# The opening of a hybrid decoder step: the next channel tile's modulation in three operations and ahead of the second block, and a residual load named later

## The chip, the cores and the metric

The kernel runs on one core of one Trainium2 chip. The metric is the device time of one launch in microseconds (us). Before the change it is 2659.37 us, the median of 3 runs that lie between 2658.36 and 2660.74.

The engines are TensorE (PE), VectorE (DVE), ScalarE (ACT), GpSimd (POOL) and SyncE (SP). In this kernel SP issues the loads and stores, all on one queue.

## The reference

One layer for a prompt of 2048 tokens and a sample group of 8 x 8 tokens, 1024 channels, in float32. Cut to what matters:

```python
mod = einsum('bd,de->be', silu(c), w_ada) + b_ada          # c: 1 prompt row, 8 sample rows
sh1, sc1, g1, sh2, sc2, g2 = split(mod, 6)
h = rmsnorm(x, norm_mix_w) * (1 + sc1) + sh1
proj = h @ w_in                                            # q k v z b a | sliding window q k v
o_dn  = gated_deltanet(proj[...])                          # short convolution first, then chunks of 64
o_swa = window_attention(proj[...])
x = x + g1 * (concat(o_dn, o_swa) @ w_out)
h = rmsnorm(x, norm_ffn_w) * (1 + sc2) + sh2
u = causal_conv3(h @ ffn_w_up) + ffn_conv_b
x = x + g2 * ((silu(gate(u)) * up(u)) @ ffn_w_down)
y = rmsnorm(x, final_norm_w)
```

The six vectors `sh1 ... g2` are the modulation; the code numbers them as components 0 to 5. Component 1 enters as `(1 + sc1) * norm_mix_w`, component 0 as an added term.

## The kernel before, in words

**Layout.** Activations stand transposed, channels on the 128 partitions in 8 channel tiles, tokens along the free dimension in blocks of up to 512. The first half of the tokens has the blocks 0 and 1, of 512 each. A product in near-float32 precision is made of three products of rounded parts: an operand is split into `hi` and `lo` (weights: `split`, L329 to L333, w_hi on ACT, w_lo on VectorE L332), and for each channel tile TensorE takes hi·w_hi, lo·w_hi and hi·w_lo (L340).

**Stages in time.** The opening (to about 70 us) computes the modulation components 0 and 1, the norm of blocks 0 and 1, and the first two column tiles of the input projection. To about 395 us follow the other columns of that projection beside components 2 to 5, to about 690 us the DeltaNet and attention mixers of the first half, then the second half, output projection, FFN up and FFN down.

**A modulation step** (`ada_load` L165, `ada_cols` L174). For one channel tile k the two 512 KB pieces of `w_ada` (components 1 and 0) are loaded, through six buffers (`WADA`). TensorE multiplies them with silu(c) (L182, `ada_ps`, the projection), ACT copies the result (L185, `ms`), TensorE transposes it (L189, `adat_ps`), and VectorE adds up four partial sums (L196) and the bias (L197) for each of the two components, and for component 1 adds 1 (L199) and multiplies by the norm's weight (L200). `ada_cols` is a generator: its first `next` makes projection and copy, the rest makes transposes and VectorE's part.

**What takes the modulation** (`affine_h`, L241). For each block and channel tile VectorE computes ht = x · S · rstd (L265). For block 0 ACT adds the shift and rounds to hi (L271), VectorE makes lo (L272). For block 1 ACT adds the shift (L267), rounds (L268), and POOL makes lo (L269).

**The norm** (`first_rstd` L296, `token_rstd` L206). ACT squares x (L302), VectorE adds tiles up (L304, L309), TensorE sums over partitions (L215, `ss_ps`), VectorE and POOL take the inverse root (L144, L145), VectorE makes diagonals (L219, `dg`), TensorE spreads the result over the partitions (L223, `rb_ps`), ACT copies it (L225, `sg`).

**The opening's loop** (L1943 on). Block 0's norm and tile 0's modulation come first. Then for each k the loop starts the loads of a further tile, `next(ada[k + 1])` (projection of tile k + 1), the steps that `PLAN[k]` lists (2: one channel tile of block 0 through `first_two`; 1: a step of block 1's norm; 3: a channel tile of block 1), and `rest(ada[k + 1])`. After it come constants (`in_consts`, L570): loads of `cw` and `dnw` (L573), the scaling of `dnw` by 0.5 on VectorE (L574), and the load of `cout` (L577). These three loads are issued behind the last `w_ada` load. POOL's copy `sb` (L553) reads what lands with `cout`.

**FFN down** (`down_phase`, L1642). In it `load_x` (L1810, load at L1816) fetches tiles of the residual; it is called in steps 1 and 5 of a phase (L1831).

**What sets the order.** The program text is the input of a scheduler that simulates the engines and writes a fixed list of instructions for each engine and for the queue. Each engine takes its list in order; an instruction that waits holds all behind it on its engine. So the source order decides only indirectly.

Of the kernel before, what the change touches and what calls it, by code (L numbers as in the profile page):

```python
# [18 lines left out]
ALU = mybir.AluOpType  # L19
# [3 lines left out]
P = 128  # L23
D = 1024
KT = 8
# [71 lines left out]
def kernel(  # L97
# [5 lines left out]
    nc = tc.nc  # L103
# [34 lines left out]
    MOD = cp.tile([P, 6, KT, 9], F32, tag="MOD", name="MOD")  # L138
    nw = cp.tile([P, 3, KT], F32, tag="nw", name="nw")
# [27 lines left out]
    def ada_load(comp, kt, wpool):  # L167
        wt = wpool.tile([P, KT, P], F32, tag="wada", name="wada", bufs=WADA)
        loads.append(nc.sync.dma_start(wt, I["w_ada"][KT * comp + kt]).ins)
        return wt  # L170

    def ada_cols(tiles, consts, wpool, bank, loaded=None):


        cT, bT = consts
        n = P * len(tiles)
        ps = bank("ada_ps")
        for q, (comp, kt) in enumerate(tiles):
            wt = loaded[q] if loaded else ada_load(comp, kt, wpool)
            for k in range(KT):  # L180
                g = k % 4
                nc.tensor.matmul(ps[32 * g:32 * g + 32, P * q:P * q + P], cT[:, k, :], wt[:, k, :],  # L182
                                 start=k < 4, stop=k >= 4, tile_position=(0, 32 * g))
        ms = wpool.tile([P, 512], F32, tag="ms", name="ms", bufs=2)
        nc.scalar.copy(ms[:, :n], ps[:, :n])  # L185
        yield True
        pt = bank("adat_ps")
        for q in range(len(tiles)):
            nc.tensor.transpose(pt[:, P * q:P * q + P], ms[:, P * q:P * q + P], ident)  # L189
        src = pt[:, :n].rearrange("p (q g r) -> p q r g", q=len(tiles), g=4)[:, :, 0:9, :]  # L190
        for comp in sorted({c for c, _ in tiles}):
            qs = [q for q, (c, _) in enumerate(tiles) if c == comp]
            k0, m = tiles[qs[0]][1], len(qs)
            dst = MOD[:, comp, k0:k0 + m, :]
            over = lambda a: a.unsqueeze(2).broadcast_to([P, m, 9])
            nc.vector.tensor_reduce(dst, src[:, qs[0]:qs[0] + m], mybir.AxisListType.X, ALU.add)  # L196
            nc.vector.tensor_tensor(dst, dst, over(bT[:, KT * comp + k0:KT * comp + k0 + m]), ALU.add)  # L197
            if comp in (1, 4):
                nc.vector.tensor_scalar_add(dst, dst, 1.0)  # L199
                nc.vector.tensor_tensor(dst, dst, over(nw[:, comp // 3, k0:k0 + m]), ALU.mult)  # L200
            elif comp == 5:
                nc.vector.tensor_scalar_mul(dst, dst, 0.5)
        yield True


# [163 lines left out]
    def rest(steps):  # L369
        for _ in steps:  # L370
            pass
# [252 lines left out]
    def bank(name, tag):  # L624
        return pm.tile([P, 512], F32, tag=tag, name=name, bufs=BANKS[tag])
# [1011 lines left out]
    def down_phase(ds, dr, pd):  # L1637
# [41 lines left out]
        w, t = {}, {}  # L1679
# [37 lines left out]
        def ahead(f):  # L1717

            while done[0] <= min(f, len(queue) - 1):
                q, i, r = queue[done[0]]  # L1720
                get_w(q, i)
                get_t(q, i, r)
                done[0] += 1
# [37 lines left out]
        for q in range(Q):  # L1761
# [3 lines left out]
            if j == 0:  # L1765
                x, sums = {}, {}
# [10 lines left out]
            def products(i, cs):  # L1777
                for m, s in cs:
                    r = subs[s]
                    n = r.stop - r.start  # L1780
                    th = t[q, i, r.start if last else 0]
                    c, v = slice(P * m, P * m + P), slice(0, n) if last else r
                    for y, (a, b) in enumerate(((0, 0), (0, 1), (1, 0))):
                        nc.tensor.matmul(acc[m, s][:, :n], w[q, i][a][:, c], th[b][:, v],  # L1784
                                         start=new and i == 0 and y == 0, stop=i == KH - 1 and y == 2,
                                         skip_group_check=True)
# [36 lines left out]
            for s in (1, 0) if last else (None,):  # L1823
                f = place[q, 0, subs[s].start] if last else f
                cs = [c for c in order if s is None or c[1] == s]
                for i in range(one):
                    ahead(f + reach(i))
                    products(i, cs)
                    if finish and i:
                        next(finish, None)  # L1830
                    if i in (1, 5):  # L1831
                        load_x()
                    if q == Q - 2 and i >= 2 and i - 2 + DR < KH:
                        get_w(Q - 1, i - 2 + DR)
                ahead(f + one - 1 + DR)
                for c in cs:
                    for i in range(one, KH):
                        products(i, [c])
                    out(*c)
                if last:  # L1840
                    rest(finish or ())
                    r = subs[s]
                    finish = norm(1, r.start, r.stop - r.start, x, sums[1], cols[1], [acc[0, 1], acc[1, 1]], True)
# [14 lines left out]
    SIDE, DR, RAWS, AHEAD = 3, 6, 4, 3  # L1858
    CV = 5
    XST, WADA = 6, 6  # L1860
    PLAN = [(2,), (2, 1), (2, 1), (2, 1, 3), (2, 3, 3), (2, 3), (2, 3, 3), (2, 3)]

    SHARE = (5.4, 2.0, 4.0, 1.9, (2.0, 1.4), 5.0, (1.3, 2.0), 8.0)
    PLAIN = 3
# [11 lines left out]
    with ExitStack() as main:  # L1876
# [9 lines left out]
        st = new_pool(first, "st", side="right")  # L1886


        with ExitStack() as es:
            ps0 = new_pool(es, "ps0", space=PSUM)  # L1890
            bank0 = lambda name: ps0.tile([P, 512], F32, tag="a", name=name, bufs=2)
            with ExitStack() as es0:
                x0 = new_pool(es0, "x0", side="right")
                xs, ada, rs = [], [], []
# [9 lines left out]
                def ada_next():  # L1904
                    k = len(ada)
                    if k == KT:
                        return
                    wts = [ada_load(c, k, st) for c in (1, 0)]
                    ada.append(ada_cols([(1, k), (0, k)], ac, st, bank0, wts))

                ac = ada_init(ip, st)
                load_x(0, 2)
# [21 lines left out]
                two = [first_two(bi) for bi in range(2)]  # L1934
# [6 lines left out]
                for k in range(KT):  # L1941
                    ada_next()
                    if k == 3:  # L1943
                        raw.append(load_raw(I["w_inT"][2]))
                    if k == 5:
                        w2 = [st.tile([P, KT, P], F32R, tag="wada", name=t, bufs=WADA) for t in ("w2_hi", "w2_lo")]
                        split(raw[2], out=w2)
                    if k + 1 < KT:
                        next(ada[k + 1])
                    for g in PLAN[k]:  # L1950
                        next((rs if g < 2 else two)[g % 2], None)
                    if k + 1 < KT:
                        rest(ada[k + 1])
                rest(two[1])
                with tc.issue_after(loads[-1]):
                    ic = in_consts(ip)
# [72 lines left out]
        with ExitStack() as es:  # L2029
            up_tags[:] = FREE_TAGS  # L2030
            filler, _ = between(0, in_end(), es, range(MU))
# [16 lines left out]
        with ExitStack() as es:  # L2048
            tq = new_pool(es, "tq", side="right")
            W = Quarters(tq)  # L2050
            q = token_quarters(h, tq)
# [115 lines left out]
```

## Time and profile before

| | |
|---|---|
| median of 3 runs | 2659.37 us (2658.36 to 2660.74) |
| the profiled execution's own time | 2657.72 us |
| its span | 2655.9 us |
| TensorE busy | 97% of the span |
| VectorE / ACT / POOL busy | 68% / 48% / 29% |
| TensorE's granted clock, mean | 0.993 |
| moved by DMA | 433.58 MB, 163 GB/s in the mean |

The span is the time from the first to the last instruction of the profiled execution; 1.8 us of its own time lie around it. The profile's lists give, for each group of instructions, start, busy time and in brackets the idle time of the engine ahead of it with the instruction that ended it. A group such as `x2` is several instructions of one kind in a row, its time that of all of them. The granted clock is a share of TensorE's full 2.4 GHz.

### The profile page before, as it was taken

The numbers are of one execution on the slowest core, as the hardware profiler recorded it, in microseconds if no ns is written. First come the engines' busy times: TensorE is split into PE (matmuls) and PEld (weight loads), VectorE is DVE, ScalarE is ACT, GpSimd is POOL, SyncE is SP. The second block draws the span as 40 slices with busy tenths as digits, with TensorE's granted clock in tenths as the row PEclk, the third lists the DMA queues.
The fourth block names the chain that finished last, engine by engine and source line by source line (L and its number), as shares of the span: only waits on it lengthen the run. The fifth ranks groups of instructions, "written<-read, shape, count | busy, mean of one in ns | idle before, by whom it ended". The sixth has DMA issues, their size and how long they took to land.

```text
span 2655.9 us, 45653 instructions
## 1 busy us (share of the span) xinstructions
PE 2581.1 (97%) x16552; PEld 2226.9 (84%) x16552; DVE 1817.5 (68%) x3681; ACT 1265.9 (48%) x3082; POOL 760.7 (29%) x643
## 2 busy tenths in 40 slices
PE   6999989999999999999999999999999998999998
PEld 5677878788998787777776789999999997889988
DVE  6466489889413687778767565886677676676676
ACT  5463265554232555445443354555555554454343
POOL 1041144343222412322121123335565520020012
PEclk9999999999999999999999999999999999999999
DMA  7687344332355243332236357414555448678673
GB/s 273 243 291 254 115 132 119 91 90 86 94 159 197 102 147 89 93 95 85 79 104 206 116 173 232 145 63 161 170 176 184 167 175 306 211 239 271 217 250 130
DMA packets 305791, 433.58 MB, mean 163 GB/s; under 512 B 81779, under 2 KB 189012, under 8 KB 305300
## 3 DMA queue, kind: packets, MB, share of 16 engines
q1 hardware_dynamic: 305564, 430.66, 49.8%
q8 instruction: 130, 2.13, 0.3%
q14 instruction: 97, 0.79, 0.1%
HBM read 316.25 MB, written 115.33 MB: 162 GB/s over the span
## 4 chain that ended last, share of the span: by engine, by line
PE 80%; DVE 8%; DMA 8%; issue 2%; ACT 1%; SPq 1%; POOL 0%; DVEq 0%; POOLq 0%; ACTq 0%
PE up_ps L340 21%; PE dn_ps L1784 14%; PE in_ps L340 12%; PE uq_b L1574 6%; PE op_ps L340 5%; PE uq_c L1574 3%; PE uq_u L1574 2%; PE uq_g L1574 2%; DMA tr<-T_d 2%; PE as_ps L959 2%; PE uq_a L1574 1%; DVE ev L548 1%; PE pv_ps L996 1%; DMA suv<-in_w_downT_dram 1%; PE am_ps L706 1%
## 5 line engine op out<-in xcount | busy, mean ns | idle before, releaser
L340 PE MATMUL in_ps<-hi,w_hi 128*128 128x512 f32 (+2 forms) x880 | 314.4, 360 | 8.4 <-DVE ev L604 4.6
L340 PE MATMUL in_ps<-lo,w_hi 128*128 128x512 f32 (+2 forms) x880 | 316.2, 359 | 3.0 <-DVE lo L272 1.7
L340 PE MATMUL up_ps<-hi,w_hi 128*128 128x512 f32 (+2 forms) x808 | 316.3, 392 | 0.0
L340 PE MATMUL in_ps<-hi,w_lo 128*128 128x512 f32 (+2 forms) x880 | 313.9, 357 | 0.0
L340 PE MATMUL up_ps<-lo,w_hi 128*128 128x512 f32 (+2 forms) x808 | 311.3, 385 | 1.1 <-DVE lo L272 1.1
L340 PE MATMUL up_ps<-hi,w_lo 128*128 128x512 f32 (+2 forms) x808 | 312.0, 387 | 0.0
L1784 PE MATMUL dn_ps<-th,wh 128*128 128x512 f32 (+2 forms) x796 | 272.4, 343 | 5.2 <-DVE x L1252 4.3
L1784 PE MATMUL dn_ps<-tl,wh 128*128 128x512 f32 (+2 forms) x796 | 272.6, 343 | 5.0 <-DVE tl L1676 5.0
L1784 PE MATMUL dn_ps<-th,wl 128*128 128x512 f32 (+2 forms) x796 | 270.7, 342 | 0.0
L332 DVE TENSOR_TENSOR w_lo<-w_raw,w_hi 128x1024 fp32r<-128x1024 f32 x115 | 144.7, 1259 | 110.6 <-ACT w_hi L331 106.5
L331 ACT CAST w_hi<-w_raw 128x1024 fp32r<-128x1024 f32 x126 | 132.0, 1047 | 167.2 <-PE op_ps L340 58.3
L340 PEld LDWEIGHTS in_ps<-hi,w_hi 128*128 128x128 f32 x880 | 164.7, 188 | 30.8 <-DVE ev L604 5.5
L340 PEld LDWEIGHTS in_ps<-lo,w_hi 128*128 128x128 f32 x880 | 165.6, 188 | 24.6 <-issue 5.4
L340 PEld LDWEIGHTS up_ps<-hi,w_hi 128*128 128x128 f32 x808 | 152.3, 188 | 37.2 <-issue 11.4
L340 PEld LDWEIGHTS up_ps<-hi,w_lo 128*128 128x128 f32 x808 | 152.0, 188 | 34.6 <-issue 6.7
L340 PEld LDWEIGHTS in_ps<-hi,w_lo 128*128 128x128 f32 x880 | 165.7, 188 | 16.9 <-issue 2.4
L340 PEld LDWEIGHTS up_ps<-lo,w_hi 128*128 128x128 f32 x808 | 152.3, 189 | 31.3 <-issue 5.1
L1784 PEld LDWEIGHTS dn_ps<-th,wh 128*128 128x128 f32 x796 | 150.7, 190 | 22.9 <-DVE x L1252 4.7
L1784 PEld LDWEIGHTS dn_ps<-tl,wh 128*128 128x128 f32 x796 | 151.0, 190 | 21.4 <-DVE tl L1676 6.1
L1784 PEld LDWEIGHTS dn_ps<-th,wl 128*128 128x128 f32 x796 | 150.9, 190 | 15.6
L1675 ACT CAST wh<-wr 128x512 fp32r<-128x512 f32 x149 | 92.0, 617 | 140.3 <-PE dn_ps L1784 108.7
L548 DVE SCALAR_TENSOR_TENSOR ev<-rb,cw,ev 128x512 f32<-128x512 f32 (+2 forms) x180 | 133.4, 747 | 19.8 <-ACT ev L541 18.6
(547 smaller groups left out, 6493.3 us busy)
## 6 DMA issues: line engine op xcount, KB each, us to landing
w_raw<-in_w_upT_dram SPq DMA_DIRECT2D x50, 512.0 KB
wada<-in_w_ada_dram SPq DMA_DIRECT2D x48, 512.0 KB
w_raw<-in_w_inT_dram SPq DMA_DIRECT2D x44, 512.0 KB
wr<-ws_d SPq DMA_DIRECT2D x88, 256.0 KB
w_raw<-in_w_outT_dram SPq DMA_DIRECT2D x34, 512.0 KB
d<-act_d SPq DMA_DIRECT2D x33, 512.0 KB
wr<-in_w_downT_dram SPq DMA_DIRECT2D x66, 256.0 KB
tr<-T_d SPq DMA_DIRECT2D x66, 256.0 KB
```

Of the source, the lines that this page charges most:

```text
L331: nc.scalar.copy(hi, raw)
L332: (eng or nc.vector).tensor_tensor(lo, raw, hi.bitcast(F32), ALU.subtract)
L340: nc.tensor.matmul(ps[:, :n], a[:, k, :], b[:, k, :n], start=first is not False and k == ks[0] and i == 0, stop=last is not False and k == ...
L548: nc.vector.scalar_tensor_tensor(out, src(j), w[:, j:j + 1], out, ALU.mult, ALU.add)
L706: nc.tensor.matmul(am_ps[:rows, h], kq[:, 2 * s + h, 0, :], kq[:, 2 * s + h], start=True, stop=True)
L959: nc.tensor.matmul(banks[v][:, 256 * g + P * k0:256 * g + 256], a[r, g0 + g], b[r, keys], start=i == 0, stop=i == 2, tile_position=(64 * v ...
L996: nc.tensor.matmul(pv_ps[64 * v:64 * v + 64, :], (vprev[0], vt)[half][:, 64 * v:64 * v + 64], PT[v, half], start=half == k0, stop=half == 1)
L1574: nc.tensor.matmul(bk[t][:, :nb], u[:, k], v[:, k], start=new and k == 0 and y == 0, stop=k == KG - 1 and y == 2, skip_group_check=True)
L1675: nc.scalar.copy(h, raw)
L1784: nc.tensor.matmul(acc[m, s][:, :n], w[q, i][a][:, c], th[b][:, v], start=new and i == 0 and y == 0, stop=i == KH - 1 and y == 2, skip_gro ...
```

## The change

It has three parts. In `ada_cols` one reduction and one bias add now take both components at once, and one `scalar_tensor_tensor` adds 1 and multiplies, so a channel tile takes three VectorE operations for six; the loads and products take component 0 ahead of 1. In the opening's loop block 0's channel tile and the transposes and VectorE part of the next tile's modulation come ahead of the steps of `PLAN`, which lists those of the second block alone. In `down_phase` the first load of the residual moves from step 1 to step 5 in the first phase (q = 0).

```diff
@@ ada_cols
-        for comp in sorted({c for c, _ in tiles}):
-            qs = [q for q, (c, _) in enumerate(tiles) if c == comp]
-            k0, m = tiles[qs[0]][1], len(qs)
-            dst = MOD[:, comp, k0:k0 + m, :]
-            over = lambda a: a.unsqueeze(2).broadcast_to([P, m, 9])
-            nc.vector.tensor_reduce(dst, src[:, qs[0]:qs[0] + m], mybir.AxisListType.X, ALU.add)
-            nc.vector.tensor_tensor(dst, dst, over(bT[:, KT * comp + k0:KT * comp + k0 + m]), ALU.add)
+        comps, ks = [sorted({t[x] for t in tiles}) for x in range(2)]
+        cs, kk = slice(comps[0], comps[-1] + 1), slice(ks[0], ks[-1] + 1)
+        n_ = len(tiles)
+        flat = lambda a: a.rearrange("p c k -> p (c k)")
+        over = lambda a: a.unsqueeze(2).broadcast_to([P, n_, 9])
+        dst = MOD[:, cs, kk, :].rearrange("p c k b -> p (c k) b") if len(comps) == 1 else MOD[:, cs, ks[0], :]
+        bias = bT.rearrange("p (c k) -> p c k", k=KT)[:, cs, kk]
+        bias = flat(bias) if len(comps) == 1 else bias[:, :, 0]
+        nc.vector.tensor_reduce(dst, src, mybir.AxisListType.X, ALU.add)
+        nc.vector.tensor_tensor(dst, dst, over(bias), ALU.add)
+        for comp in comps:
+            scale = MOD[:, comp, kk, :]
             if comp in (1, 4):
-                nc.vector.tensor_scalar_add(dst, dst, 1.0)
-                nc.vector.tensor_tensor(dst, dst, over(nw[:, comp // 3, k0:k0 + m]), ALU.mult)
+                nc.vector.scalar_tensor_tensor(scale, scale, 1.0, nw[:, comp // 3, kk].unsqueeze(2).broadcast_to([P, len(ks), 9]),
+                                               ALU.add, ALU.mult)
             elif comp == 5:
-                nc.vector.tensor_scalar_mul(dst, dst, 0.5)
+                nc.vector.tensor_scalar_mul(scale, scale, 0.5)
@@ down_phase
-                    if i in (1, 5):
+                    if i == 5 or i == 1 and q:
                         load_x()
@@ the opening
-    PLAN = [(2,), (2, 1), (2, 1), (2, 1, 3), (2, 3, 3), (2, 3), (2, 3, 3), (2, 3)]
+    PLAN = [(), (1,), (1,), (1, 3), (3, 3), (3,), (3, 3), (3,)]
...
-                    wts = [ada_load(c, k, st) for c in (1, 0)]
-                    ada.append(ada_cols([(1, k), (0, k)], ac, st, bank0, wts))
+                    wts = [ada_load(c, k, st) for c in (0, 1)]
+                    ada.append(ada_cols([(0, k), (1, k)], ac, st, bank0, wts))
...
                     if k + 1 < KT:
                         next(ada[k + 1])
+
+                    next(two[0])
+                    if k + 1 < KT:
+                        rest(ada[k + 1])
                     for g in PLAN[k]:
                         next((rs if g < 2 else two)[g % 2], None)
-                    if k + 1 < KT:
-                        rest(ada[k + 1])
```

The lists of the engines move at three places that matter. In them `x_125` and `x_142` are the tokens of block 0 and block 1, a projection of 32 products stands as x16, and lines from L206 on are six higher after the change.

TensorE in the opening, from the projection of tile 3 to that of tile 5. Before:

```order
L182 MATMUL ada_ps<-wada,cT 32x128 x16
L215 MATMUL ss_ps<-ones,xst 128x1 x8
L340 MATMUL in_ps<-hi,w_hi 128x512 x2
L189 MATMUL adat_ps<-cst,ms 128x128 x2
L340 MATMUL in_ps<-lo,w_hi 128x512
L340 MATMUL in_ps<-hi,w_lo 128x512
L340 MATMUL in_ps<-lo,w_hi 128x512
L340 MATMUL in_ps<-hi,w_lo 128x512
L182 MATMUL ada_ps<-wada,cT 32x128 x16
L223 MATMUL rb_ps<-dg,ones 128x128 x4
L340 MATMUL in_ps<-hi,w_hi 128x512 x2
```

After the change:

```order
L182 MATMUL ada_ps<-wada,cT 32x128 x16
L346 MATMUL in_ps<-hi,w_hi 128x512 x2
L189 MATMUL adat_ps<-cst,ms 128x128 x2
L221 MATMUL ss_ps<-ones,xst 128x1 x8
L346 MATMUL in_ps<-lo,w_hi 128x512
L346 MATMUL in_ps<-hi,w_lo 128x512
L346 MATMUL in_ps<-lo,w_hi 128x512
L346 MATMUL in_ps<-hi,w_lo 128x512
L182 MATMUL ada_ps<-wada,cT 32x128 x16
L346 MATMUL in_ps<-hi,w_hi 128x512
L346 MATMUL in_ps<-lo,w_hi 128x512
```

Tile 2's two hi products and tile 3's transposes now stand ahead of the sums over partitions of block 1's norm (`ss_ps`), which stood first; and the spreading of its result (`rb_ps`), which followed tile 4's projection at once, now comes behind six products and tile 4's transposes.

VectorE from tile 4's modulation to the split of a weight tile. Before:

```order
L196 TENSOR_REDUCE MOD<-adat_ps 128x9 x2
L197 TENSOR_TENSOR MOD<-MOD,bT 128x9 x2
L199 TENSOR_SCALAR MOD<-MOD 128x9
L200 TENSOR_TENSOR MOD<-MOD,nw 128x9
L265 SCALAR_TENSOR_TENSOR ht<-x_125,MOD,sg 128x512
L265 SCALAR_TENSOR_TENSOR ht<-x_142,MOD,sg 128x512 x2
L574 TENSOR_SCALAR dnw<-dnw 128x1
L332 TENSOR_TENSOR w_lo<-w_raw,w_hi 128x1024
L272 SCALAR_TENSOR_TENSOR lo<-ht,MOD,hi 128x512
```

After the change:

```order
L200 TENSOR_REDUCE MOD<-adat_ps 128x2x9
L201 TENSOR_TENSOR MOD<-MOD,bT 128x2x9
L580 TENSOR_SCALAR dnw<-dnw 128x1
L205 SCALAR_TENSOR_TENSOR MOD<-MOD,nw 128x9
L271 SCALAR_TENSOR_TENSOR ht<-x_142,MOD,sg 128x512
L271 SCALAR_TENSOR_TENSOR ht<-x_125,MOD,sg 128x512
L271 SCALAR_TENSOR_TENSOR ht<-x_142,MOD,sg 128x512 x2
L338 TENSOR_TENSOR w_lo<-w_raw,w_hi 128x1024
L278 SCALAR_TENSOR_TENSOR lo<-ht,MOD,hi 128x512
```

The scaling of `dnw`, which stood behind tile 4's modulation and three ht, now stands ahead of the last operation of that modulation and of all four ht.

SP's queue at the start of the FFN's down phase. Before:

```order
L1485 DMA E_d<-d_18627 128x1088
L1816 DMA x_22573<-x2T 128x4x512
L1669 DMA tx<-act_d 128x512 x4
L1669 DMA wr<-in_w_downT_dram 128x512
L1669 DMA tr<-act_d 128x512
```

After the change:

```order
L1491 DMA E_d<-d_18601 128x1088
L1822 DMA x_22655<-x2T 128x4x512
L1675 DMA tx<-act_d 128x512 x4
L1675 DMA wr<-in_w_downT_dram 128x512
L1675 DMA tr<-act_d 128x512
```

The load of the residual has not moved in the queue. Besides these places the lists differ in the mixers of the first half, about 395 to 690 us, where the scheduler has laid the same instructions of all engines in another sequence; from there on they are the same.

## Rows read from the trace of the kernel before

**Rows 1.** The page's first part: for each engine busy time, its share of the span and the number of instructions.

```profile
PE 2581.1 (97%) x16552; PEld 2226.9 (84%) x16552; DVE 1817.5 (68%) x3681; ACT 1265.9 (48%) x3082; POOL 760.7 (29%) x643
```

**Rows 2.** Busy time by stretch: the stretch, its length, then for PE, its weight loads, DVE, ACT and POOL the busy time with the number of instructions, the granted clock, the DMA share, GB/s.

```profile
28.60:48.60 20.00, 15.92 (x186) 11.53 (x182) 15.46 (x43) 10.64 (x20) 3.81 (x4) 0.91 0.83 282
48.60:69.30 20.70, 19.17 (x105) 13.77 (x106) 17.73 (x34) 11.58 (x24) 8.89 (x7) 1.00 0.47 169
395.00:690.00 295.00, 287.80 (x2430) 242.38 (x2429) 263.17 (x773) 151.90 (x544) 110.02 (x92) 1.00 0.33 97
```

**Rows 3.** VectorE's timeline in the opening: start, us, the instructions, and in brackets the idle time ahead of them with what ended it.

```profile
20.89 0.30 DVE L196 TENSOR_REDUCE MOD<-adat_ps 128x9 f32<-128x36 f32 x2 [0.79 <-PE adat_ps L189]
21.43 0.17 DVE L199 TENSOR_SCALAR MOD<-MOD 128x9 f32<-128x9 f32 x1
21.63 0.17 DVE L200 TENSOR_TENSOR MOD<-MOD,nw 128x9 f32<-128x9 f32 x1
...
33.77 0.75 DVE L265 SCALAR_TENSOR_TENSOR ht<-x,MOD,sg 128x512 f32<-128x512 f32 x1
...
36.10 0.16 DVE L144 TENSOR_SCALAR rsq<-ss_ps 128x4 f32<-128x4 f32 x1
37.45 0.88 DVE L219 TENSOR_SCALAR dg<-cst,rtok 128x128 f32<-128x128 f32 x4 [1.19 <-POOL rtok L145]
38.24 0.29 DVE L196 TENSOR_REDUCE MOD<-adat_ps 128x9 f32<-128x36 f32 x2
...
43.09 2.08 DVE L265 SCALAR_TENSOR_TENSOR ht<-x,MOD,sg 128x512 f32<-128x512 f32 x3
45.33 0.15 DVE L574 TENSOR_SCALAR dnw<-dnw 128x1 f32<-128x1 f32 x1 [0.16 <-DMA dnw<-in_dn_norm_w_dram]
...
48.70 1.15 DVE L199 TENSOR_SCALAR MOD<-MOD 128x9 f32<-128x9 f32 x1
...
60.23 0.30 DVE L196 TENSOR_REDUCE MOD<-adat_ps 128x9 f32<-128x36 f32 x2 [2.37 <-PE adat_ps L189]
```

**Rows 4.** TensorE's timeline in the opening, and as the last row one from the start of the down phase; columns as in rows 3.

```profile
32.72 1.46 PE L182 MATMUL ada_ps<-wada,cT 128*32 128x128 f32 x32
34.11 1.95 PE L215 MATMUL ss_ps<-ones,xst 128*128 128x1 f32 x16
35.92 0.72 PE L340 MATMUL in_ps<-hi,w_hi 128*128 128x512 f32 x2
36.48 0.38 PE L189 MATMUL adat_ps<-cst,ms 128*128 128x128 f32 x2
...
46.89 0.73 PE L340 MATMUL in_ps<-hi,w_hi 128*128 128x512 f32 x2
48.61 0.50 PE L340 MATMUL in_ps<-lo,w_hi 128*128 128x512 f32 x1 [0.99 <-POOL lo L269]
...
64.85 0.50 PE L340 MATMUL in_ps<-lo,w_hi 128*128 128x512 f32 x1 [0.66 <-DVE lo L272]
...
69.05 0.39 PE L340 MATMUL in_ps<-hi,w_lo 128*128 128x512 f32 x1
69.28 0.40 PE L340 MATMUL in_ps<-hi,w_hi 128*128 128x512 f32 x1
...
2206.51 0.79 PE L1784 MATMUL dn_ps<-tl,wh 128*128 128x512 f32 x1 [4.69 <-DVE tl L1676]
```

**Rows 5.** ACT's timeline in the opening; columns as in rows 3.

```profile
24.45 3.23 ACT L302 ACTIVATE xst<-x 128x512 f32<-128x512 f32 x6
...
34.56 0.72 ACT L271 ACTIVATE hi<-ht,MOD 128x512 fp32r<-128x512 f32 x1 [3.44 <-DVE ht L265]
...
40.85 0.59 ACT L225 COPY sg<-rb_ps 128x512 f32<-128x512 f32 x1
```

**Rows 6.** The chain of waits that ends at 49 us: start, us, what held.

```profile
37.78 1.05 PE ada_ps L182 x32
...
40.34 5.41 DMA cout<-in_state_dn_convT_dram
```

**Rows 7.** Busy time of TensorE alone in three stretches: the stretch, its length, busy time with the number of products, the granted clock, the DMA share, GB/s.

```profile
30.40:33.80 3.40, 3.40 (x33) 0.54 0.98 374
43.80:45.00 1.20, 0.00 (x0) 1.00 0.79 231
2202.00:2212.00 10.00, 5.18 (x13) 0.66 0.85 306
```

**Rows 8.** TensorE's waits between 395 and 690 us, the first of the list: us in all, times, the longest.

```profile
PE kq_ps L667 <- DVE AM L708: 1.7, 1, 1.7
```

**Rows 9.** TensorE's timeline where products of the input projection follow other products; columns as in rows 3.

```profile
385.82 0.42 PE L340 MATMUL in_ps<-hi,w_hi 128*128 128x384 f32 x1
386.08 0.33 PE L340 MATMUL in_ps<-lo,w_hi 128*128 128x384 f32 x1
386.25 0.34 PE L340 MATMUL in_ps<-hi,w_lo 128*128 128x384 f32 x1
```

**Rows 10.** SP's timeline at the start of the down phase: start and duration of the issues.

```profile
2191.73 0.32 SPq L1485 DMA_DIRECT2D E_d<-d  x1
2192.14 0.42 SPq L1816 DMA_DIRECT2D x<-x2T  x1
2192.61 2.84 SPq L1669 DMA_DIRECT2D tx<-act_d  x4
```

## The prediction

> **What bounds the kernel now.** I read the page's busy shares first: TensorE is busy 97% of the span, VectorE 68% [rows 1]. So a VectorE instruction that goes away is worth time only where TensorE stands still, and the next view is busy time by stretch [rows 2]. TensorE lacks 4.1 us in 28.6 to 48.6, 1.5 in 48.6 to 69.3, and 7.2 in 395 to 690. The edit lies in the opening, that is in the first two of these. The timeline of VectorE there [rows 3] shows one modulation step as two reductions, two adds, a +1 and a product, then the affine product ht. The timeline of TensorE [rows 4] shows what follows from it: the hi products wait for ht by way of ACT [rows 5]. The chain of waits [rows 6] shows a second thread: the last w_ada load is issued when TensorE is through with tile 4's projection (38.83), behind it on the same queue come cw, dnw and cout, and cout's landing releases POOL's sb copy and the first lo product of the second block. VectorE meets dnw at 45.33 and waits 0.16 us, so dnw lands at 45.3 [rows 3].
>
> **What the three operations save.** From the first reduction of a tile at 20.89 to where ht could start, 21.63 + 0.17 = 21.80, a step takes 0.91 us [rows 3]. A small operation that depends on the one before starts 0.20 after it (21.43 to 21.63). Three in a row give 0.60, so a step is shorter by 0.3 us, not by half, since the two reductions overlapped, 0.30 us for the pair, and the two adds behind them were through by 21.43. The Trainium skill (VectorE: DVE Perf Modes, "The DRAIN you can't avoid") says that the next operation waits until the pipe is empty and to cut the count; by that six operations to three would save a full half of the step. The rows show pairs that overlap, and 0.3 stands. Over eight tiles that is 2.4 us of VectorE; whether TensorE gets it depends on the order.
>
> **Steps of the opening, in the new order.** Tile 0's ht waits for sg, which no modulation speeds, and gains nothing. For tile 1, ht is 0.3 early, ACT's hi is not (ACT squares x until 27.7 [rows 5]), lo is, by 0.3. So the transposes of tile 2 and its modulation start 0.3 earlier, and ht, a step that is 0.3 shorter later, comes at 33.1 for 33.77 [rows 3].
> TensorE now takes tile 2's hi products and tile 3's transposes ahead of the eight sums of squares. Tile 3's projection ends at about 33.8 (34.18 less 0.33) [rows 4], hi is there at 33.1 + 0.79 + 0.72 = 34.6 [rows 5]: TensorE stands 0.8 us where before the sums filled the place. Hi products and transposes take 0.9 us (35.92 to 36.86), and tile 3's modulation starts at 35.5 for 38.24. Then come sums 1.9, four products at 0.23, tile 4's projection 1.05 [rows 4, 6]: done at 39.4, not 38.83. That is 0.55 us late, and w_ada, cw, dnw and cout with it: dnw lands at 45.3 + 0.55 = 45.85.
> VectorE does lo of tile 3 until 38.4, then rsq, which it did at 36.10 before; the wait for POOL (1.19) and dg (0.88) follow, so the second block's row sums are spread 2.3 us later, and its sg stands at about 42.6 for 41.44 [rows 5].
> Now the costly place. The new order has dnw **between the add and the last operation of tile 4's modulation**, with four ht and w_lo behind it. Tile 4's transposes come after its projection (39.4) and six products (1.4), at 41.05; VectorE's first two operations end at about 41.5, and then it stands until 45.85: **4.3 us in place of 0.16**. Before, it used that time for ht and three more ht (43.09, 2.08 us). Behind VectorE wait ACT (hi of tile 4, ht of the second block), POOL (lo of the second block) and TensorE, which has only tiles 5 and 6's projections left: it runs dry at about 44.9 (the broadcast of rstd 1.2, two projections of 1.05, ACT's copy between). dnw and the last operation take 0.35, two ht 1.4, ACT's bias, hi and cast 0.7 + 0.7 + 0.6 (partly beside them): TensorE resumes at 48.5 to 48.9. Before, it began its corresponding work at 46.89, so it is **about 2 us behind** here.
> What is left to the end of the first four sums of columns is the same work: 72 products at 0.23 (69.05 to 69.28), one projection 1.05, four transposes 0.44, in sum 18.1 us. Before, it took 69.28 - 46.89 = 22.4 us for nearly that, with waits for lo of POOL and of VectorE (0.99 and 0.66 are the longest [rows 4]) and first products after a wait that start the next one late. In the new order tile 7's transposes stand ten products earlier, VectorE's wait of 2.37 us at 60.23 goes, and the second block's ht no longer stand ahead of a modulation. POOL still delays small VectorE operations (1.15 us for one of 0.17, at 48.70): two per step now, three before. I leave 1.0 us of waits for the first lo of POOL: 48.8 + 18.1 + 1.0 = 67.9, for 69.28. That is 1.4 us early; I take **1.2**, since the row at 48.70 shows that POOL can cost one more hold. Bounds: no wait left and resumption at 48.5 give -2.7; two more holds of 1.15 give +1.0.
>
> **Clock.** The granted clock was 0.54 from 30.4 to 33.8 and 0.66 in the mean from 2202 to 2212 [rows 7], about a stand of 4.69 us that ended at 2206.51 [rows 4]: most of those ten us at the lower level, 1.2 GHz. A stand of 1.2 us (43.8 to 45.0) left it at 1.00. The new stand is 3.6 to 4 us. The Trainium skill (TensorE: Matmul & The Clock Gate, "HAM oscillation") says that such stands throw the clock back to the low level and the next matmuls run cold. The row at 2206.51 agrees. In the sum I keep the full clock, since after the stand TensorE waits for POOL anyway; the low clock is a rival below.
>
> **The mixers of the first half, 395 to 690.** The diff does not name them, but the recorded order of all engines differs there: the same 2,200 instructions, sequenced anew. Nothing in the rows says which sequence waits less. TensorE's waits there are 7.2 us, the longest 1.7 [rows 8]: below, they could all go (-7.2); above, the like could come again (+7). One thing can be counted: the changes between in_ps products and other matmuls on TensorE fall from 199 to 187 in the two lists, six fewer entries. An entry costs 0.26 to the next product, not 0.17 [rows 9]: 6 x 0.09 = **0.5 us saved**. For the waits I take nothing.
>
> **The residual load of down.** In source it moves from step 1 to step 5. In the issuing queue it stands where it stood: behind the last E_d, ahead of four tx loads, with the same waits; before, it is issued at 2192.14 and the tx loads at 2192.61 [rows 10]. Price: nothing, either way. **The other modulation steps** (components 2 to 5, 83 to 395) lose two VectorE operations of 0.2 us before 395 us; VectorE is idle a third of the time [rows 1], which covers them: nothing. From 690 on the order is the same on every engine, so what is gained earlier is carried to the end.
>
> **Sum.** -1.2 - 0.5 = -1.7 us against the profiled execution, 2657.72 us (span 2655.9 and 1.8 around it), which is 1.65 below the median. Against the median: 2659.37 - 1.7 = **2657.7 us**.
>
> **Rivals.**
> A. *The stand at dnw brings the low clock* (slower). If the granted clock falls for a stretch as long as that at 30.4 (3.4 us), TensorE loses half of it, 1.7; if as long as that from 2202 to 2212 (a mean of 0.66 is 6.8 us of ten at one half), 3.4. Opening: +0.5 to +2.2, total 2659.4 to 2661.1; I put it at **2660.4**. It decides from 2.4 us of low clock under work on (1.2 / 0.5). For: the stand is close to 4.69 us [rows 4]. Against: the stand of 1.2 us that ended at 45.0 left the clock at 1.00 [rows 7], and 48.6 to 69.3 has 1.00 throughout [rows 2]. By the page of the Trainium skill named above this would be the likelier case. Chance 0.22.
> B. *The mixers' new sequence removes most waits*: -1.2 - 0.5 - 5 gives **2652.7**. For: the waits are many and short, and each has independent products that could stand in front. Against: the first sequence came from the same scheduler. Chance 0.14.
> C. *The new sequence adds waits*: +5 or more, **2663 to 2666**. Chance 0.07.
> D. *dnw does not hold VectorE* (it lands early or the stand is filled): the 2 us behind TensorE's resumption go, **2655.7**. Against: the load stands behind 1 MB of w_ada on the queue and cannot go sooner than tile 4's projection. Chance 0.05.
> E. *The part on the residual load does nothing*: held for certain above, and without price.
>
> **How the numbers follow.** Forecast 0.52, A 0.22, B 0.14, C 0.07, D 0.05. A difference under 0.2% (5.3 us) cannot be told from none in a measurement of this kernel; the runs shown spread over 2.4 us. Faster by that means under 2654.05: most of B and little of the forecast, 0.14. Slower means over 2664.7: half of C and the tail of A, 0.05. The rest, 0.81, is no change. The range reaches from B, 2652.7, to the upper end of A with the mixers 1.5 us worse, 2662.6, and leaves out half of B and most of C.
>
> **What would show it.** Right: in 20 to 70, one reduction, one add and one fused operation per tile, 0.6 us together; a wait of VectorE for dnw's load of 3.5 to 5 us near 41.5; TensorE without work near 45 to 48.5; few TensorE waits from 50 to 68; the start of the product that stood at 69.28 near 68; the x load in the same place before the tx loads. Wrong: a wait for dnw under 1 us; a granted clock of one half after 48 (A); the modulation of tile 7 still waiting for its transposes; TensorE's idle time in 395 to 690 outside 4 to 10 us (B, C); any difference after 690 that is more than a shift.

## The result and the profile after the change

The changed kernel takes **2672.11 us**, the median of 4 runs (2669.32 to 2673.13), against 2658.86 us for the kernel before (4 runs): a ratio of 1.0041, interval [1.0024, 1.0058]. It is slower: by 0.41% in that ratio, some 11 us; the two medians differ by 13.3 us (0.50%). Run again later beside other kernels (run 6 below), the ratio was 1.0044 [1.0030, 1.0059]. The forecast, 2657.7 us in a range up to 2662.6, is wrong.

The profiled execution took 2673.13 us (span 2671.3), 15.4 us over that of before. The latter was one of the quick ones: in the later comparisons single runs of the kernel before lie between 2655.6 and 2671.3 us, around medians of 2660 to 2662. One profile against another is thus good to a few us, and the ratios carry the verdicts.

The same three stretches as [rows 2], after the change (stretch, length, busy time and count of PE, weight loads, DVE, ACT, POOL, granted clock, DMA share, GB/s):

```profile
28.60:48.60 20.00, 16.39 (x149) 12.57 (x145) 8.30 (x22) 6.44 (x12) 1.01 (x1) 0.74 0.75 253
48.60:69.30 20.70, 18.19 (x121) 13.27 (x122) 18.32 (x27) 11.09 (x19) 9.53 (x7) 0.84 0.43 146
395.00:690.00 295.00, 282.11 (x2270) 235.94 (x2268) 267.42 (x761) 152.33 (x543) 107.99 (x91) 0.98 0.32 92
```

TensorE is busy in the opening as before, but it gets less done: the clock there is 0.74 and 0.84 for 0.91 and 1.00. "Low clock" below means time at the lower of its two levels, 1.2 GHz for 2.4. In the mixers TensorE stands without work for 12.9 us, not 7.2.

VectorE in the opening, the answer to [rows 3] (start, us, instructions, idle time ahead and what ended it):

```profile
20.87 0.23 DVE L200 TENSOR_REDUCE MOD<-adat_ps 128x18 f32<-128x72 f32 x1 [0.79 <-PE adat_ps L189]
21.14 0.18 DVE L201 TENSOR_TENSOR MOD<-MOD,bT 128x18 f32<-128x18 f32 x1
21.35 0.17 DVE L205 SCALAR_TENSOR_TENSOR MOD<-MOD,nw 128x9 f32<-128x9 f32 x1
...
45.96 0.18 DVE L201 TENSOR_TENSOR MOD<-MOD,bT 128x18 f32<-128x18 f32 x1
49.02 0.15 DVE L580 TENSOR_SCALAR dnw<-dnw 128x1 f32<-128x1 f32 x1 [2.87 <-DMA dnw<-in_dn_norm_w_dram]
49.09 0.16 DVE L205 SCALAR_TENSOR_TENSOR MOD<-MOD,nw 128x9 f32<-128x9 f32 x1
49.51 2.77 DVE L271 SCALAR_TENSOR_TENSOR ht<-x,MOD,sg 128x512 f32<-128x512 f32 x4 [0.26 <-issue]
```

A step is 0.65 us long (20.87 to 21.52) in place of 0.91. The wait for dnw stands inside tile 4's modulation, as the order said, and the four ht behind it.

TensorE, the answer to [rows 4]:

```profile
34.44 1.02 PE L346 MATMUL in_ps<-hi,w_hi 128*128 128x512 f32 x2 [1.84 <-ACT hi L277]
35.26 0.63 PE L189 MATMUL adat_ps<-cst,ms 128*128 128x128 f32 x2
35.68 3.41 PE L221 MATMUL ss_ps<-ones,xst 128*128 128x1 f32 x16
...
51.76 2.07 PE L346 MATMUL in_ps<-hi,w_hi 128*128 128x512 f32 x4 [1.75 <-ACT hi L277]
54.59 0.79 PE L346 MATMUL in_ps<-lo,w_hi 128*128 128x512 f32 x1 [0.76 <-POOL lo L275]
...
74.65 0.40 PE L346 MATMUL in_ps<-hi,w_hi 128*128 128x512 f32 x1
```

The product that started at 69.28 starts at 74.65: the opening is **5.4 us late**. The sums over partitions take 3.41 us for 1.95 [rows 4]; that, too, is the clock, for in run 6, where it is full there, they take 1.84. Work at the lower level thus takes nearly twice as long, and half of a stretch of low clock is used below as an estimate of what it costs. TensorE alone in four stretches (stretch, length, busy time, clock, DMA share, GB/s):

```profile
34.60:44.60 10.00, 10.00 (x60) 0.51 0.48 169
52.00:58.00 6.00, 5.24 (x29) 0.50 0.54 200
478.00:482.00 4.00, 3.95 (x14) 0.57 0.24 33
574.00:582.00 8.00, 8.00 (x35) 0.57 0.41 124
```

Ten us at 1.2 GHz follow the stand of 1.84 us at 34.44, and six more the stand of 1.75 at 51.76. Before, the opening had 3.4 us of it [rows 7]. The other two stretches lie in the mixers, where the profile of before has none: the first starts where TensorE has stood 2.2 us for Y.

TensorE's waits between 395 and 710 us, the answer to [rows 8] (us in all, times, the longest):

```profile
PE p_ps L859 <- DVE xz L917: 3.7, 2, 3.1
PE u_ps L786 <- DVE Y L834: 2.5, 2, 2.2
PE kq_ps L673 <- DVE AM L714: 1.6, 3, 0.9
PE uu_ps L846 <- DVE o L868: 1.5, 1, 1.5
PE vt_ps L948 <- ACT pt L994: 1.2, 1, 1.2
```

None of these was among the long ones before. The mixers can be timed between two issues of the queue that every version has, the four loads of G near 390 us and the store of `out_p_swa_k` near 801. Two rows of the kernel before, then two of the change (the loads by the timeline: start and us; the store by its tile: ns of one, first and last start):

```profile
389.81 1.39 SPq L722 DMA_DIRECT2D G<-at_d  x4
```

```profile
L612 SPq DMA_DIRECT2D out_p_swa_k_dram<-ev x1: 425/425/425, 800.8 to 800.8; - x1
```

```profile
396.56 1.39 SPq L728 DMA_DIRECT2D G<-at_d  x4
```

```profile
L618 SPq DMA_DIRECT2D out_p_swa_k_dram<-ev x1: 423/423/423, 817.9 to 817.9; - x1
```

That is 411.0 us before and 421.3 after: **10.3 us** of the 15.4 are lost here. The opening has 5.4, the part between 1.4 (6.75 at the loads of G less 5.4), and 1.7 come back behind 801.

The residual load, the answer to [rows 10]:

```profile
2209.15 0.32 SPq L1491 DMA_DIRECT2D E_d<-d  x1
2209.56 0.41 SPq L1822 DMA_DIRECT2D x<-x2T  x1
2210.02 2.80 SPq L1675 DMA_DIRECT2D tx<-act_d  x4
```

It is issued where it was, 0.41 us behind the last E_d, both times.

### The profile page after: what moved, and what is told of

Read it like the earlier page. It is cut to its first block, busy times and chain, and to the rows that moved or that the text cites. A ratio compares the mean times of both kernels' runs of the same rounds, so it can differ in the third digit from the quotient of the medians.

```text
span 2671.3 us, 45633 instructions
## 1 busy us (share of the span) xinstructions
PE 2595.9 (97%) x16552; PEld 2240.2 (84%) x16552; DVE 1823.9 (68%) x3655; ACT 1267.1 (47%) x3082; POOL 758.7 (28%) x643
## 5 line engine op out<-in xcount | busy, mean ns | idle before, releaser
L1682 DVE TENSOR_TENSOR wl<-wr,wh 128x512 fp32r<-128x512 f32 x149 | 108.8, 730 | 55.3 <-ACT wh L1681 51.5
```

Of the source, the lines that this page charges most:

```text
L1682: nc.vector.tensor_tensor(l, raw, h.bitcast(F32), ALU.subtract)
```

## The experiments

Two theories stood against rivals. **Clock**: the opening's loss is low clock, behind the stand at dnw and behind the hi products that were moved. **List**: the mixers' loss belongs to the new sequence that the scheduler wrote for them, not to what they take over from the opening. A useful fact: the scheduler gives the mixers one of a few lists, so versions can be built that share one part's list, word for word on TensorE, and differ in the other. Call the mixers' list of before B, that of the change A, a third C.

**1. The three operations alone.** The old loop, PLAN and load_x with the new `ada_cols`:

```diff
 (before)
-        for comp in sorted({c for c, _ in tiles}):
...
+        nc.vector.tensor_reduce(dst, src, mybir.AxisListType.X, ALU.add)
+        nc.vector.tensor_tensor(dst, dst, over(bias), ALU.add)
...
+                nc.vector.scalar_tensor_tensor(scale, scale, 1.0, ...)
...
+                    wts = [ada_load(c, k, st) for c in (0, 1)]
```

> The three operations alone: loop, PLAN and load_x as before. TensorE's list in the opening has the sums over partitions ahead of tile 2's hi products again, VectorE's has dnw behind the four ht, and the mixers' list differs from that of before in some 80 places only. Theory (the loss of the change is one of clock in the opening, about 5 us, and one of the mixers' new list, about 10 us): neither is there, so the total is 0 to 3 us under before, 2656 to 2659. Rival (the wide reduction or the fused operation is itself at fault): the opening is late by several us, total 2664 or more.

Ratio 1.0009 [0.9998, 1.0020]: no difference that can be told, and not the gain that the theory named. The profile's opening is 1.7 us early with no low clock in it at all. TensorE there and in the mixers (columns as above):

```profile
28.60:70.00 41.40, 37.26 (x305) 1.00 0.65 226
395.00:700.00 305.00, 297.84 (x2446) 0.97 0.33 92
```

Its mixers took 419.0 us, 8.0 over before, on B's list but for a few entries near its start, and with TensorE standing 7.2 us as before; 17.1 us of low clock lie there, half of which makes up the 8. So the three operations are not at fault, and low clock comes and goes between executions by more than I had allowed.

**2. The new loop with the six old operations.**

```diff
 (before)
-    PLAN = [(2,), (2, 1), (2, 1), (2, 1, 3), (2, 3, 3), (2, 3), (2, 3, 3), (2, 3)]
+    PLAN = [(), (1,), (1,), (1, 3), (3, 3), (3,), (3, 3), (3,)]
...
+                    next(two[0])
+                    if k + 1 < KT:
+                        rest(ada[k + 1])
                     for g in PLAN[k]:
                         next((rs if g < 2 else two)[g % 2], None)
-                    if k + 1 < KT:
-                        rest(ada[k + 1])
```

> The new loop and PLAN with the six old operations. TensorE's list in the opening is word for word that of the change, and dnw stands inside tile 4's modulation; the mixers have a third list. Theory: the opening is 5 to 8 us late at 80 us, with two stretches of low clock from about 34 and about 52 us; what the mixers cost depends on the third list, between 0 and +10. Rival (the loss in the opening comes with the three operations): the opening within 1 us of before.

Ratio 1.0022 [1.0011, 1.0033]. VectorE and TensorE at the stand, and TensorE's clock (columns as above):

```profile
46.45 0.15 DVE L574 TENSOR_SCALAR dnw<-dnw 128x1 f32<-128x1 f32 x1 [4.41 <-DMA dnw<-in_dn_norm_w_dram]
49.02 1.73 PE L340 MATMUL in_ps<-hi,w_hi 128*128 128x512 f32 x4 [3.17 <-ACT hi L271]
```

```profile
34.60:44.80 10.20, 8.78 (x110) 1.00 0.68 221
50.00:56.00 6.00, 4.90 (x31) 0.50 0.44 155
```

The stand is as large as forecast (4.41 us, 4.3 in the prediction) and the low clock follows it; but the first stretch, expected from 34 us on, is not there. The opening is 3.3 us late, not 5 to 8. List C has no long wait.

**3. The change without the stand.** One word, with every other list as in the change:

```diff
 (changed kernel)
-        nc.vector.tensor_scalar_mul(d["dnw"], d["dnw"], 0.5)
+        nc.gpsimd.tensor_scalar_mul(d["dnw"], d["dnw"], 0.5)
```

> The changed kernel with the scaling of dnw on POOL, ahead of the sb copy that waits for the later load anyhow; all other lists are word for word those of the change. Theory (two clock losses in the opening, only the second made by the stand at dnw): the low clock from 34 us on stays, that from 52 goes, the opening is 2 to 4 us earlier than in the change, and the mixers lose the same 10 us, total 2667 to 2670. Rival 1 (the stand makes all of the opening's loss): the opening is level with before, total 2665 to 2667. Rival 2 (the mixers lose because of what they take over from the opening, not by their list): their loss moves by more than 3 us.

Ratio 1.0040 [1.0027, 1.0053]: the loss is the same. TensorE's clock at 34.6 and behind the place of the stand, and its longest waits in the mixers:

```profile
34.60:44.80 10.20, 10.20 (x60) 0.51 0.50 169
50.00:58.00 8.00, 6.71 (x61) 1.00 0.84 272
```

```profile
PE p_ps L859 <- DVE xz L917: 3.6, 2, 2.9
PE kq_ps L673 <- DVE AM L714: 2.8, 3, 1.4
PE uu_ps L846 <- DVE o L868: 1.9, 1, 1.9
PE u_ps L786 <- DVE Y L834: 1.8, 2, 1.6
```

The second stretch of low clock is gone, the first stays, and the opening is 2.8 us late for 5.4. The mixers have list A's waits again and take 423.8 us (loads of G at 392.57, store at 816.4). They began 4 us earlier than in the change, so what they take over from the opening is not what makes them slow.

**4. The change with dnw at the very start.** Its load stands behind that of nw; TensorE's list in the opening is that of the change, the mixers' list is C:

```diff
 (changed kernel)
-        nc.vector.tensor_scalar_mul(d["dnw"], d["dnw"], 0.5)
+        d["dnw"] = dnw0
...
                 nc.sync.dma_start(nw, I["normT"])
+                dnw0 = ip.tile([P, 1], F32, tag="dnw", name="dnw")
+                nc.sync.dma_start(dnw0, I["dn_norm_w"])
+                nc.vector.tensor_scalar_mul(dnw0, dnw0, 0.5)
                 ada_next()
```

> The changed kernel with dnw loaded and scaled at the very start. TensorE's list in the opening is word for word that of the change; the mixers have the third list, the same as in order_only. Theory: the opening as in dnw_on_pool; the mixers' time the same as in order_only to within 1.5 us, since it is the list that sets it. Rival (mixers lose by what they take over): their time here is that of the opening's, so between those of dnw_on_pool and before.

Ratio 1.0002 [0.9989, 1.0014], TensorE's longest waits in the mixers:

```profile
PE u_ps L786 <- DVE Y L834: 1.2, 1, 1.2
PE z_ps L786 <- DVE T L807: 0.8, 1, 0.8
```

This is the cleanest pair. Runs 3 and 4 have the same operations but for the place of dnw, the same opening on TensorE and no stand at dnw; both reach the mixers at the same time (loads of G at 392.57 and 392.41). With list A these take 423.8 us, with C 415.5 (store at 807.9), and run 2, which has list C too, takes 415.2. The pair differs by 8.3 us in the profiles, of which half of the low clock makes 3.4 (13.7 us of it against 6.8); the medians differ by 6.8 us (2671.05, 2664.24), and the intervals of the two ratios lie apart. The list is what costs.

**5. The residual load alone.**

```diff
 (before)
-                    if i in (1, 5):
+                    if i == 5 or i == 1 and q:
```

> The later residual load alone: all lists are word for word those of before, so it also is a second profile of before. Both theories: the same time to within 0.1%. What it tells besides is the low clock: if its stretches are set by the list alone, the granted clock is low where it was in the profile of before (30 to 34, 374 to 386, 1436 to 1444, 2204 to 2212, 37 us in all); if they come and go from execution to execution, some 5 to 30 us of others stand beside them, and the time differs by half of that.

Ratio 1.0003 [0.9994, 1.0013]: nothing. As a second profile of the same lists it shows a wait of 1.7 us for AM as in [rows 8] and one of 1.7 for PT, which was 1.3 before, and 53.9 us of low clock in all where the first profile has 37.1.

**6. The change again,** unaltered.

> The changed kernel once more, beside the others on one chip. Theory (its mixers' list holds waits of its own): the waits of TensorE stand where they stood, near 478 (u_ps), 524 (p_ps, 3 us), 556, 560 and 686, and the time from 390 to 800 us is 9 to 14 us over before, of which 5 to 7 are waits and the rest half of the low clock there. Rival (chance of one execution): those waits are gone or elsewhere, and the time from 390 to 800 within 4 us of before. Total 2668 to 2674 by the theory.

Ratio 1.0044 [1.0030, 1.0059]. The stand, TensorE's clock and its waits:

```profile
44.67 0.15 DVE L580 TENSOR_SCALAR dnw<-dnw 128x1 f32<-128x1 f32 x1 [3.01 <-DMA dnw<-in_dn_norm_w_dram]
```

```profile
34.60:44.80 10.20, 9.13 (x118) 1.00 0.80 250
48.00:56.00 8.00, 6.41 (x36) 0.59 0.55 183
```

```profile
PE p_ps L859 <- DVE xz L917: 3.1, 1, 3.1
PE uu_ps L846 <- DVE o L868: 1.8, 1, 1.8
PE u_ps L786 <- DVE Y L834: 1.6, 1, 1.6
```

The three longest waits recur, those at 556 and 560 us do not. The mixers take 417.7 us (392.24 to 809.9), 6.7 over before: less than the 9 I had named, so the range was too narrow. The first stretch of low clock is absent this time, the one behind the stand is there, and the opening is 1.4 us late.

**7. List C behind the old opening.** Six operations, old loop, dnw scaled on POOL:

```diff
 (before)
-        nc.vector.tensor_scalar_mul(d["dnw"], d["dnw"], 0.5)
+        nc.gpsimd.tensor_scalar_mul(d["dnw"], d["dnw"], 0.5)
```

> The kernel before with the scaling of dnw on POOL: old loop, six operations, TensorE's opening the same up to its last column tiles, but the mixers have the third list, that of order_only and dnw_early. Theory (the list sets the mixers' time): 390 to 800 us as in those two, 0 to 4 us over before by the profile with half of the low clock counted in, waits near 514 (u_ps, 1.2 us) and 604 to 608; total within 3 us of before. Rival (the mixers suffer from the late opening): level with before, and not like those two.

Ratio 1.0007 [0.9996, 1.0018]; mixers 413.6 us (391.33 to 804.9), the longest wait u_ps with 1.2 us as in run 4. List C carries its waits with it, whatever the opening.

**8. A fifth list.** The changed kernel with the two loads of each step swapped back:

```diff
 (changed kernel)
-                    wts = [ada_load(c, k, st) for c in (0, 1)]
+                    wts = [ada_load(c, k, st) for c in (1, 0)][::-1]
```

> The changed kernel with the loads of the two pieces of w_ada in the old order (component 1 first), the products in the new: it alters the opening a little and gives the mixers a fifth list. It tells whether the list is a draw: theory, the mixers' waits are neither those of the change nor those of before, and the time from 390 to 800 lies anywhere from 0 to +12 us; total 2660 to 2672. Rival (the new opening itself makes the mixers slow): +9 to +14 us there, as in the change.

Ratio 1.0019 [1.0010, 1.0027]. Its opening is the best of all, 2.6 us early without low clock, and its mixers give that back: a new wait of 3.5 us for xz at 551 and 2.7 us for Y at 599, 422.6 us in all (387.38 to 810.0). It has 17.1 us of low clock in the mixers, so not all of that is waits. Which list comes out is a draw as far as these versions show: it is not aimed at by the edit.

**9. Two versions meant to beat both:** the three operations in the old loop, once with the loads swapped as in run 8, once with dnw at the start as in run 4. Both have list C.

> The three operations in the old loop, with the loads of w_ada in the old order. No long wait for dnw (it stands behind the four ht and w_lo), the sums over partitions ahead of tile 2's hi products, and the mixers have the third list, the one without long waits. Theory (stand, place of the sums and list made the loss): the opening 1 to 3 us ahead of before at 80 us, 390 to 800 us as in third_list_old_opening, total 2657 to 2661, at or up to 3 us under before. Rival (every change of list costs): 2664 or more.

> The three operations in the old loop, with dnw loaded and scaled at the start; the mixers have the third list. Theory: as in three_ops_old_load_order, total 2657 to 2661. Rival: 2664 or more.

Ratios 1.0004 [0.9992, 1.0016] and 1.0018 [1.0009, 1.0027]. Their openings are 0.6 and 1.8 us early, but neither is faster than the kernel before; the second is slower, against the theory and in the rival's range, and I cannot say why.

**10. What the stand costs.** Run 2 again, and run 2 with dnw scaled on POOL, all other lists alike:

> order_only once more, as the partner of new_loop_no_stand on one chip: new loop, six operations, the third list, dnw inside tile 4's modulation. A wait of VectorE for dnw of 3 to 5 us, TensorE without work for 2 to 3 us behind it and then the low clock for about 6.6 us, as in the three profiles with the stand so far. Total 0.1 to 0.3% over before. Rival (the low clock there is chance): full clock from 48 to 58.

> order_only with the scaling of dnw on POOL; every other list is word for word the same, so the stand at dnw is all that differs from new_loop_stand. Theory (the stand and the low clock behind it cost 2 to 5 us): full clock from 48 to 58, 2 to 5 us under new_loop_stand. Rival (the stand costs nothing, since TensorE then waits for POOL anyhow): the same time to within 1.5 us.

Ratios 1.0019 [1.0008, 1.0030] and 1.0022 [1.0010, 1.0033]: no difference in the time. In the profiles the opening is 3.8 us late with the stand and 0.2 early without, and behind 48 us stand 6.8 us of low clock against 3.4. TensorE's waits there, two rows with the stand, then one without:

```profile
49.52 1.24 PE L340 MATMUL in_ps<-hi,w_hi 128*128 128x512 f32 x4 [2.18 <-ACT hi L271]
52.35 0.79 PE L340 MATMUL in_ps<-lo,w_hi 128*128 128x512 f32 x1 [1.59 <-POOL lo L269]
```

```profile
49.22 0.76 PE L340 MATMUL in_ps<-lo,w_hi 128*128 128x512 f32 x1 [2.35 <-POOL lo L269]
```

Without the stand TensorE still waits 2.35 us for POOL, as the rival said, against 3.77 with it. The opening as a whole has 13.7 us of low clock with the stand and 3.4 without. Half of that difference is 5.1 us, more than the 4.0 between the two openings; 3.4 of it lie ahead of the stand, which cannot have made them. So of the 4.0 no more than some 0.6 us is left to the stand in these two profiles, and the totals show no cost that can be told. What it costs stays open.

**The mixers in all fourteen profiles.** From the loads of G to the store: the length, TensorE's time without work, its low clock, and the rest, which is the length less the time without work and half of the low clock (us; an estimate).

| list | profiles | length | without work | low clock | rest |
|---|---|---|---|---|---|
| A | the change, run 6, run 3 | 421.3, 417.6, 423.8 | 13.5, 10.3, 14.7 | 10.2, 10.2, 13.7 | 402.7, 402.3, 402.3 |
| B | before, run 5 | 411.0, 412.9 | 7.6, 7.2 | 0, 3.4 | 403.4, 404.0 |
| B but for a few entries | run 1 | 419.0 | 8.6 | 17.1 | 401.9 |
| C | runs 2, 4, 7, 9 (two), 10 (two) | 413.4 to 417.7 | 6.1 to 7.9 | 0 to 10.2 | 405.1 to 406.2 |
| a fifth | run 8 | 422.6 | 11.0 | 17.1 | 403.1 |

The time without work goes with the list. The low clock does not: run 1 has nearly B's list and more of it than any profile of A, and run 8 as much. That list A brings more of it is thus not shown. Nor does the mixers' list settle the total by itself: the seven runs with list C have ratios from 1.0002 to 1.0022, some 5 us apart, and what moves them is not shown. The three with list A have 1.0040 to 1.0044, above all others.

## Why the prediction was wrong

- **Bound and place.** TensorE sets the time, and the two places named, the opening and the mixers, are where it was lost. Right.
- **What the operations save.** 0.3 us a step forecast, 0.26 measured (0.91 less 0.65). Alone they change nothing (run 1). Right.
- **The stand at dnw.** 4.3 us forecast; 2.87, 3.01, 3.42 and 4.41 us in the four profiles that have it, with dnw landing at 49.0 in the change, 44.7 in run 6, 46.5 in run 2 and 47.0 in run 10 (45.85 forecast). Right in place and cause; three of the four are under the 3.5 us that the prediction named as the least.
- **The opening without the clock.** -1.2 us forecast. With half of the low clock taken off on both sides, the change is at 5.4 - (17.1 - 3.4) / 2 = -1.5 in its first profile and at 1.4 - (6.8 - 3.4) / 2 = -0.3 in run 6, run 3 at 2.8 - (10.2 - 3.4) / 2 = -0.6, run 4 at 2.2 - (10.2 - 3.4) / 2 = -1.2. The forecast fits these; but by the same sum run 2 is at +1.6 and its second execution in run 10 at -1.3, so the sum is good to some 3 us and no proof.
- **Keeping the full clock after the stand.** This step failed. The sum put the low clock there at nothing; all four profiles with the stand have 6.8 us of it behind the stand, some 3.4 us of TensorE's time by half. Of those with the new opening and no stand two have none and one has 3.4. It was rival A, with 0.22, at +0.5 to +2.2, and 3.4 was the upper end of its price; the opening was late by 1.4 and 5.4 us in the two profiles of the change, the 5.4 with the early stretch below in it. TensorE did not stand for the 3.6 to 4 us that were forecast, but for 1.75, 1.86, 2.18 and 3.17 us for ACT's hi, and again for 0.76 to 1.59 us for POOL's lo. The Trainium skill (TensorE: Matmul & The Clock Gate, "HAM oscillation") has long waits of TensorE followed by a slow clock; the trace agrees, here with a shorter one: 0.50 from 52 to 58 us behind a stand of 1.75.
- **The early stretch.** I took the low clock at 30 to 34 over from [rows 7] as it was. In the new order, with the hi products ahead of the sums, it was 10 us in three of seven profiles, 6.8 in one, and absent in three; with the sums first 3.4 in four of seven and absent in three. In the change and in run 3 TensorE had stood 1.84 us ahead of it, in the three profiles of the new order without it 1.60 to 1.63 at the same place. Why it comes in one execution and not in the next is not shown.
- **The mixers.** This is the step that made the sign wrong. I took -0.5 from six fewer changes of product and nothing for the waits, and gave rival C, waits of the new list, 0.07. By the table above the mixers with list A are 6.6 us longer in the mean than with B and in run 1: 5.0 of that is time without work, 2.3 half of the low clock, and -0.7 the rest. So C's mechanism was right, and so was its price for the waits, +5; the low clock I had not priced, and whether it belongs to the list is not shown. With the opening's 1.4 to 5.4 us this makes most of the 11 us in the totals. The count of changes says nothing of the waits: list C has some 50 more than list A and stands less. But the rest in the table is largest with C, 405.1 to 406.2 us, where the changes are most numerous, and for A the forecast of -0.5 stands beside the -0.7.
- **The residual load.** No effect forecast, none found (run 5). Right.
- **From 690 on only a shift.** The lists are alike, and 17.1 us at 801 became 15.4 at the end. Right within what executions differ by.

## What to carry to other kernels

Where a scheduler writes the order, an edit of one stage also draws a new list for stages far away, and that draw can outweigh the edit: here some 5 us of waits in the mixers by the profiles, and 6.8 us between the medians of runs 3 and 4, against about -1 in the opening without its clock. Compare the lists first, and where a stage that the edit does not name differs, give that both signs and a real chance. Give low clock a range of its own: in run 6 6.8 us of it follow a wait of 3.1 us for xz, and in the change and run 3 none follows that wait at once. To judge the edit itself, look for a variant whose far stage has the old list (or one list in common), and compare those.

## What the runs showed of the hardware

The granted clock varies between executions of one program, and with it the time. Between 358 and 390 us all fourteen profiles have 10 to 17 us of the lower level, and near 1440 7 to 10. Others are in one profile and not in another of the same lists: run 5 has 3.4 us at 240 and 3.4 at 434, and the profile of before has neither. In all it is 37.1 and 53.9 us for these two, 71.9 and 55.1 for the two of the change, counted to the end of the clock's record, some 2 us past the span. In 29 runs of the kernel before on one chip the time lay between 2656.58 and 2671.28 us, the mean clock between 0.992 and 0.987.
